# Gate product of an encoder block: one more k-pair of the second half formed by seven products, and three k-pairs held back to the end instead of four

## The chip, the cores and the metric

The kernel is one program on one core of a Trainium2 chip. The metric is the device time of one execution in microseconds (us), the median over several runs. All times inside an execution are counted from the start of its profiled span.

## The reference, cut to what matters

One layer of an encoder on x (256 tokens x 2048 channels, float32): a state-space and pooling mixer, a gated convolutional MLP, and last a gated embedding. Only this last step is touched:

```
gate = sigmoid(rmsnorm(h, ple_norm_pre) @ w_ple_gate)     # 256 x 2048 @ 2048 x 2048
h = h + rmsnorm(gate * (p @ w_ple), ple_norm_post)
```

## The kernel before, in words

**Stages.** In time order: input projection and mixer, output projection, the MLP's *up* product (11264 columns, 300 to 786 us), its *down* product (786 to 1008), and the *gate* product (from 1020). Each product runs in float32 accuracy by three passes: every operand x is split into a high part (a cast on ACT, line 153) and a low part (x minus the high part, on DVE, line 154), and PE adds high x high, high x low and low x high.

**The gate product** is `token_major`, called once for each half of the 1024 output columns (lines 1140 to 1152). The outputs of a half are four PSUM banks of 128 tokens x 512 columns, acc[t][o] for t = 0, 1 (tokens) and o = 0, 1 (columns). The 2048 input channels are 16 blocks of 128, taken in pairs: a pair k covers blocks k and k+1. `gt_ks` gives the order of the blocks, so u counts the pairs in that order.

- A *plain* pair is one load of 1 MB (`raw`, ring of three buffers), two splits of 128x1024 and 24 matmuls of 128x512 (2 blocks x 2 t x 2 o x 3 passes).
- A *fast* pair (`gt_fast` lists its u) is Winograd's form of a 2x2 block product: seven products instead of eight, 21 matmuls (`seven_products`, line 255). It needs two block sums of the weights and four sums of the activations. The weights' part that is needed as it is, 0.75 MB, goes to `raw` (tile gt18r for pair 8 of half 1), the block sums, 1 MB, to a *page* (gt18t). They are split in four pieces: a (128x512), b, d and c (128x1024 each). a and b come from r, d and c from t.
- After the last fast pair one more pair follows, and then `combine` (line 283) adds the products together on DVE and changes the accumulators in place. In half 1 it also cuts acc[1][1] in two outputs of 256 columns.
- With `tail` = n, the last n pairs are *held back*: their splits are made as they come, and their matmuls run at the end, output by output, so that the first tokens' outputs are complete while PE still works on the other tokens. In half 1 `tail` is 4.
- Held-back pairs must keep their splits. Those of the plain rings hold five tiles; for two of the four pairs of half 1 four pages are set aside (`spare`, lines 1148 to 1151).

**Block sums** are made during up (`block_sums`, line 226): a job fetches 1 MB of weights into a page (SP's queue), adds blocks in place on DVE (four additions of 128x512, line 253), and stores the page to DRAM (POOL's queue). The up product is cut in 176 pieces of 16 matmuls; the job with number i is fetched at piece `46 * i // 10 + 4` and added and stored three pieces later (lines 923 to 927). 37 jobs: 32 for down, 5 for gate. The last two in the list, those of the first two fast pairs of down, stay in their pages.

**Activations' sums** (`Sums`, line 808) are made on first use and kept, two pairs to a page: psp8 holds those of pairs 8 and 10, psp12 those of pair 12.

**Pages** are a pool of 13 tiles of 128x2048. A page is taken when its tile is first written and free after its last use, so the list of tiles also sets which load waits for what.

**The finish** (lines 1153 to 1178, `finish`, line 1119): for each output a tanh on ACT (L1163), a product with pl (L1164, DVE), the sum of squares (L1171, ACT) and a product with a gain (L1172, DVE). Here pl[0], the tile plb, serves half 0. When all outputs of a token group are there, POOL makes the reciprocal root (L378, L381) and DVE scales and adds h, four pieces of 512 (L1135). For the second token group the last output's sum of squares closes the norm (L1169, with a number from L1117), then POOL L1122, ACT L1126, one product on PE (line 1127, into the bank `gof` that line 1177 has filled with h), ACT L1129, and the stores.

**Order.** In up an order written out by hand (`in_order`) holds ACT, DVE and SP to the program's order. Elsewhere a scheduler orders each engine; each engine and each DMA queue then works in that order, so a load that waits for its buffer holds up the loads behind it.

Of the kernel before, what the change touches and what calls it, by code (L numbers as in the profile page):

```python
# [20 lines left out]
NK = D // P  # L21
# [32 lines left out]
def build(nc, a, out):  # L54
# [3 lines left out]
    w_down, w_gate, w_ple = a["w_down"], a["w_gate"], a["w_ple_"]  # L58
    out = out[0]

    with tile.TileContext(nc) as tc, \
# [21 lines left out]
        def main(name):  # L83
            return [pm.tile([P, 512], F32, tag="main", name=f"{name}_{i}") for i in range(2)]

        def misc(name):
            return pc.tile([P, 512], F32, tag="misc", name=name)

        def mm(o, lhsT, rhs, start, stop):
            last["pe"] = ins(nc.tensor.matmul(o, lhsT, rhs, start=start, stop=stop, skip_group_check=True))  # L90
# [15 lines left out]
        acc, acc2 = [main(f"dtu{t}") for t in range(2)], main("dtu2")  # L106
# [50 lines left out]
        def raw(name, src=None):  # L157
            r = wp.tile([P, 2048], F32, tag="raw", bufs=3, name=name)
            if src is not None:
                last["dma"] = load(r, src, True)  # L160
            return r
# [57 lines left out]
        def columns(acc):  # L219

            c = 0
            for o in acc:
                yield o, c
                c += o.shape[-1]
# [30 lines left out]
        def seven_products(name, stage, w, k0, c0, a_, acc, alt, start, stop):  # L255

            if (stage, c0, k0) in sums_:
                r = raw(f"{name}r")  # L260
                last["dma"] = load(r[:, 512:], w[c0 // 1024, k0 // 2][:, 512:], True)
                t, held = sums_[stage, c0, k0]
                if not held:
                    t = page(f"{name}t")
                    last["dma"] = load(t, sums_[stage, c0, k0][0], True)
            else:
                r = t = raw(f"{name}r", w[c0 // 1024, k0 // 2])
            b11 = split(f"{name}a", r[:, 512:1024], 512)
            b2 = split(f"{name}b", r[:, 1024:], 1024)
            if r is t:  # L270
                add_blocks(r)
            t42 = split(f"{name}d", t[:, 1024:], 1024)
            t31 = split(f"{name}c", t[:, :1024], 1024)

            for x, (wh, wl), c, o, own in (
                    ("a11", b11, 0, alt[0], True), ("a12", b2, 0, acc[0][0], False), ("a22", t42, 0, acc[1][0], False),
                    ("s4", b2, 512, acc[0][1], False), ("s2", t42, 512, alt[3], True), ("s1", t31, 512, alt[1], True),
                    ("s3", t31, 0, alt[2], True)):
                xh, xl = a_[x]
                for q, (xx, ww) in enumerate(((xh, wh), (xh, wl), (xl, wh))):  # L280
                    mm(o, xx, ww[:, c:c + 512], own and start and q == 0, own and stop and q == 2)
# [23 lines left out]
        def token_major(name, w, c0, ks, get, acc, tail=1, fast=(), alt=None, sums=None, at=()):  # L305


            group, nu = [], len(ks) // 2
            for u in range(nu):
                if u in at:  # L310
                    at[u]()
                k0 = ks[2 * u]
                if u in fast:
                    if u == fast[0]:
                        alt = alt + [misc(f"{name}s{i}") for i in (2, 3)]
                    seven_products(f"{name}{k0}", name[:2], w, k0, c0, sums(k0), acc, alt, u == fast[0], u == fast[-1])
                    continue
                r = None if f"{name}{k0}_0" in ready else raw(f"{name}r{k0}", w[c0 // 1024, k0 // 2])
                for j in range(2):
                    group.append((k0 + j, *split(f"{name}{k0}_{j}", r and r[:, j * 1024:(j + 1) * 1024], 1024)))  # L320
                if nu - tail <= u < nu - 1:
                    continue

                order = [(t, o, g, q) for t in range(2) for o in columns(acc[t]) for g in group for q in range(3)] \
                    if u == nu - 1 or u - 1 in fast[-1:] else \
                    [(t, o, g, q) for g in group for t in range(2) for q in range(3) for o in columns(acc[t])]
                for t, (o, c), (k, wh, wl), q in order:
                    xh, xl = (v[:, t * P:(t + 1) * P] for v in get(k))
                    xx, ww = ((xh, wh), (xh, wl), (xl, wh))[q]
                    c = (c + 512 * (k + 1)) % 1024  # L330
                    mm(o, xx, ww[:, c:c + o.shape[-1]], k == ks[0] and q == 0, k == ks[-1] and q == 2)
                if u - 1 in fast[-1:]:
                    combine(name, acc, alt, nu - tail == u + 1 and tail > 1)
                group = []
                aside()
            if nu in at:
                at[nu]()
# [116 lines left out]
        for u in range(0, NK, 2):  # L454
# [20 lines left out]
            for j in range(2):  # L475
# [3 lines left out]
                if k == 8:  # L479
                    half = last["act"], last["dve"]  # L480
# [428 lines left out]
            h_kept.append(dp.tile([P, D], F32, tag=f"h{t}", bufs=1, name=f"h_kept{t}"))  # L909
        pl_kept = dp.tile([P, D], F32, tag="pl", bufs=1, name="pl_kept")  # L910

        dn_fast, gt_fast = ((2, 3, 4, 5, 7, 8, 9, 10, 11, 12, 13, 14, 15, 16, 17, 18, 19), (2, 3, 4, 5, 7, 8, 9, 11, 12, 13, 14, 15, 16, 18, 19)), ((4, 5, 6), (1, 2))

        dn_stored = (2, 3, 5, 7, 8, 10, 11, 13, 14, 16, 17, 18, 19)
        gt_ks = list(range(NK)), [0, 1, 8, 9, 10, 11, 2, 3, 4, 5, 6, 7, 12, 13, 14, 15]
        which = [("dn", w_down, c * 1024, 2 * u) for c in range(2) for u in dn_fast[c]] + \
            [("gt", w_gate, c * 1024, gt_ks[c][2 * u]) for c in range(2) for u in gt_fast[c]]
        jobs_at = [[] for _ in range(NPIECES)]
# [3 lines left out]
        jobs_at[6].append(lambda: load(pl_kept, pl[0]))  # L922
        for i, w_ in enumerate(which[2:] + which[:2]):
            fetch, add, store = block_sums(*w_, i >= len(which) - 2)
            n = 46 * i // 10 + 4
            jobs_at[n].append(fetch)
            jobs_at[n + 3].extend((add, store))
        hid, kept = [], {}
# [87 lines left out]
        with in_order():  # L1016
            for _ in range(5):
                next_part()
            for n in range(NPIECES):
                s, v, i = blocks[n // 4]  # L1020
                if n % 4 == 0:
                    acc = main(f"{'gv'[v]}a{s}{i}")
# [60 lines left out]
        def first():  # L1083
# [3 lines left out]
            for j in range(2):  # L1087
# [4 lines left out]
        hp = sublayer("dn", w_down, list(range(NF)), hid_get, gload("gffn", a["ffn_norm_post"][0]), h, V_PN,  # L1092
                      fast=dn_fast, sums=hid_sums, at={11: first, NF // 2: lambda: (ple_parts(), back())}, row=rf)
# [45 lines left out]
        hps = Sums("ps", hp)  # L1139
        for half in range(2):  # L1140

            alt = [] if half else main(f"gts{half}")
            acc = [main(f"gt{half}{t}") for t in range(2)]
            alt += main(f"gts{half}") if half else []
            ks, fast = gt_ks[half], gt_fast[half]
            if half == 1:

                for i in (8, 10):
                    sh, sl = page(f"gth{i}", F32R), page(f"gtl{i}", F32R)
                    for j in range(2):  # L1150
                        spare[f"gt1{ks[i]}_{j}"] = (sh[:, j * 1024:(j + 1) * 1024], sl[:, j * 1024:(j + 1) * 1024])
            token_major(f"gt{half}", w_gate, half * 1024, ks, hp, acc, 1 + 3 * half, fast, alt, hps)
            for t in range(2):
                for n, (o, c0) in enumerate(columns(acc[t])):
                    c1 = c0 + o.shape[-1]
                    c = slice(half * 1024 + c0, half * 1024 + c1)

                    th = mid(f"gth{half}{t}{n}")
                    v = th[:, :c1 - c0]
                    end = half == t == 1 and c1 == 1024  # L1160
                    if end:
                        rest_of(th[:, c1 - c0:c1 - c0 + 1])
                    nc.scalar.activation(v, o, AF.Tanh, scale=rh[t])  # L1163
                    nc.vector.scalar_tensor_tensor(v, v, 1.0, pl[half][:, t * 1024 + c0:t * 1024 + c1],  # L1164
                                                   op0=ALU.add, op1=ALU.mult)
                    q = tiny(f"gq{t}{half}{n}", 1)
                    sv, so = (th[:, a_:a_ + c1 - c0 + end] for a_ in (0, 512))
                    if end:
                        nc.scalar.activation(so, sv, AF.Square, scale=D ** -0.5, accum_out=q)  # L1169
                    else:  # L1170
                        nc.scalar.activation(so, sv, AF.Square, accum_out=q)  # L1171
                    nc.vector.tensor_mul(vg[t][:, c], v, gple[:, c])  # L1172
                    sq[t].append(q)
                if half == 1:
                    if t == 0:
                        last_ps = misc("gof")
                        mm(last_ps, ident, h[1][:, :512], True, False)
                    finish(t)
# [72 lines left out]
```

## Time and profile before

| | us |
|---|---|
| runs, median (lowest to highest) | 1116.56 (1115.88 to 1116.61) |
| profiled execution | 1116.13 |
| its span, first to last instruction | 1114.4 |
| PE busy in the span | 1104.0 (99%) |
| DVE busy | 959.6 (86%) |
| ACT busy | 723.8 (65%) |
| POOL busy | 69.0 (6%) |

The time of an execution is some 1.7 us longer than its span. PE is TensorE, PEld its weight loads, DVE VectorE, ACT ScalarE, POOL GpSimd, SP the engine that issues most DMAs; a q behind a name (SPq) is the sequencer that issues or waits. A row of a timeline gives the start, the duration, the engine, the line of the kernel, the operation and `out<-in` with the tiles' names, where buffer numbers are left out: `gt` stands for all accumulators of the gate product, `gt1r` for the loads of plain pairs of half 1, `gt110t` for t of pair 10 of half 1. A bracket behind it names the idle time ahead of it and what ended that. Matmuls overlap, so PE's pace is the distance of their starts, not their durations.

### The profile page before, as it was taken

To read this page: it belongs to the slowest core of one execution; us is meant where nothing else is said; L and a number is where in the kernel's file an instruction comes from. 1 tells how busy PE (TensorE), PEld (TensorE's weight loads), DVE (VectorE), ACT (ScalarE), POOL (GpSimd) and SP (SyncE) were. 2 spreads that over 40 slices of the span, in tenths; PEclk is the share of its full clock that TensorE was granted. 3 is DMA by queue.
4 is the path that set the end of the run, shared out by engine and by line. 5 is a ranking of instruction groups with operands and counts; after the bars stand their busy time and mean duration, and the time that the engine had idled before them with its cause. 6 is when DMAs were issued, how large, how long until landed. Compare 5 with 4: busy or idle time off the path is not lost.

```text
span 1114.4 us, 16061 instructions
## 1 busy us (share of the span) xinstructions
PE 1104.0 (99%) x5964; PEld 950.6 (85%) x5964; DVE 959.6 (86%) x1338; ACT 723.8 (65%) x1056; POOL 69.0 (6%) x140
## 2 busy tenths in 40 slices
PE   9999999999999999999999999999999999999997
PEld 9999988888888888888888888888888888877876
DVE  6568997899868998888888888888899999989895
ACT  6858763555775565664655655657689878767673
POOL 0200000100100000000000000000000000001001
PEclk9999999999999999999999999999999999999999
DMA  9753346454589999999899999999999899995662
GB/s 363 314 204 137 117 188 263 151 189 178 195 343 397 382 396 385 361 378 374 335 378 385 356 377 366 352 393 391 362 382 381 322 348 403 415 378 222 265 235 105
DMA packets 54943, 347.29 MB, mean 312 GB/s; under 512 B 6096, under 2 KB 6992, under 8 KB 20176
## 3 DMA queue, kind: packets, MB, share of 16 engines
q1 hardware_dynamic: 44064, 289.53, 66.8%
q0 software_dynamic: 10368, 56.10, 13.3%
q8 instruction: 47, 0.77, 0.3%
q10 hardware_dynamic: 432, 0.62, 0.2%
q14 instruction: 32, 0.26, 0.1%
HBM read 297.48 MB, written 48.76 MB: 311 GB/s over the span
## 4 chain that ended last, share of the span: by engine, by line
PE 94%; DVE 2%; ACT 2%; issue 1%; POOL 1%; DMA 0%; SPq 0%; POOLq 0%; ACTq 0%
PE ga L90 22%; PE va L90 22%; PE dna L90 12%; PE woa L90 7%; PE xbc L90 5%; PE gt L90 5%; PE z L90 4%; PE dns L90 4%; PE dtu L90 4%; PE dn0s L90 2%; PE dn1s L90 2%; PE yd L90 1%; PE pw L90 1%; PE gts L90 1%; PE ple L90 1%
## 5 line engine op out<-in xcount | busy, mean ns | idle before, releaser
L90 PE MATMUL ga<-wox,ug_0h 128*128 128x512 f32 x352 | 125.5, 395 | 0.0
L90 PE MATMUL ga<-wox,ug_1h 128*128 128x512 f32 x352 | 125.1, 394 | 0.0
L90 PE MATMUL va<-wox,uv_1h 128*128 128x512 f32 x352 | 124.8, 393 | 0.0
L90 PE MATMUL va<-wox,uv_0h 128*128 128x512 f32 x352 | 124.8, 393 | 0.0
L90 PE MATMUL ga<-wox,ug_1l 128*128 128x256 f32 x352 | 99.1, 282 | 0.0
L90 PE MATMUL va<-wox,uv_1l 128*128 128x256 f32 x352 | 99.1, 281 | 0.0
L90 PE MATMUL va<-wox,uv_0l 128*128 128x256 f32 x352 | 99.1, 281 | 0.0
L90 PE MATMUL ga<-wox,ug_0l 128*128 128x256 f32 x352 | 99.0, 281 | 0.0
L253 DVE TENSOR_TENSOR dnb<-dnb 128x512 f32<-128x512 f32 x128 | 88.3, 690 | 3.1
L90 PEld LDWEIGHTS va<-wox,uv_1h 128*128 128x128 f32 x352 | 66.1, 188 | 15.0
L90 PEld LDWEIGHTS ga<-wox,ug_1h 128*128 128x128 f32 x352 | 66.1, 188 | 15.0
L90 PEld LDWEIGHTS va<-wox,uv_0h 128*128 128x128 f32 x352 | 66.1, 188 | 15.0
L90 PEld LDWEIGHTS ga<-wox,ug_0h 128*128 128x128 f32 x352 | 66.1, 188 | 14.9
L90 PEld LDWEIGHTS ga<-wox,ug_0l 128*128 128x128 f32 x352 | 66.2, 188 | 0.1
L90 PEld LDWEIGHTS ga<-wox,ug_1l 128*128 128x128 f32 x352 | 66.2, 188 | 0.0
L90 PEld LDWEIGHTS va<-wox,uv_0l 128*128 128x128 f32 x352 | 66.2, 188 | 0.0
L90 PEld LDWEIGHTS va<-wox,uv_1l 128*128 128x128 f32 x352 | 66.2, 188 | 0.0
L937 ACT CAST hs<-hid 128x512 fp32r<-128x512 f32 x44 | 27.3, 621 | 21.8 <-PE dna L90 21.6
L244 POOL DMA_DIRECT2D dns<-dnb x30 | 16.2, 541 | 310.9 <-DVE dnb L253 310.9
L938 DVE TENSOR_TENSOR hs<-hid,hs 128x512 fp32r<-128x512 f32 x44 | 30.2, 686 | 5.8 <-ACT hs L937 5.8
L801 ACT CAST he<-he 128x512 fp32r<-128x512 f32 x13 | 8.1, 621 | 37.7 <-DVE he L800 37.7
L90 PE MATMUL dna<-dn_1h,hs 128*128 128x512 f32 x96 | 30.9, 393 | 0.0
(2247 smaller groups left out, 3227.7 us busy)
## 6 DMA issues: line engine op xcount, KB each, us to landing
dnb<-w_down SPq DMA_DIRECT2D x32, 1024.0 KB, 9.8
dns<-dnb POOLq DMA_DIRECT2D x30, 1024.0 KB, 6.6
hd<-hsum POOLq DMA_DIRECT2D x24, 512.0 KB, 8.3
zr<-w_z SPq DMA_DIRECT2D x8, 1024.0 KB, 4.9
dtur<-w_dtu SPq DMA_DIRECT2D x14, 528.0 KB, 8.6
wo0r<-w_out_ SPq DMA_DIRECT2D x7, 1024.0 KB, 4.9
dn1r<-w_down SPq DMA_DIRECT2D x7, 1024.0 KB, 6.8
hsum<-he POOLq DMA_DIRECT2D x13, 512.0 KB, 7.7
```

The source lines that it names most:

```text
L90: last["pe"] = ins(nc.tensor.matmul(o, lhsT, rhs, start=start, stop=stop, skip_group_check=True))
L244: nc.gpsimd.dma_start(t, pg[0])
L253: nc.vector.tensor_add(v[:, i], v[:, i], v[:, j])
L801: nc.scalar.copy(o[:, :512], s[:, :512])
L937: nc.scalar.copy(t[:, :512], hid_part(k))
L938: nc.vector.tensor_sub(t[:, 512:], hid_part(k), t[:, :512].bitcast(F32))
```

## The change

```
-        dn_fast, gt_fast = (...), ((4, 5, 6), (1, 2))
+        dn_fast, gt_fast = (...), ((4, 5, 6), (1, 2, 3))
...
-        gt_ks = list(range(NK)), [0, 1, 8, 9, 10, 11, 2, 3, 4, 5, 6, 7, 12, 13, 14, 15]
+        gt_ks = list(range(NK)), [0, 1, 8, 9, 10, 11, 12, 13, 2, 3, 4, 5, 6, 7, 14, 15]
...
-            n = 46 * i // 10 + 4
+            n = 45 * i // 10 + 4
...
-                for i in (8, 10):
+                for i in (10,):
                     sh, sl = page(f"gth{i}", F32R), page(f"gtl{i}", F32R)
                     for j in range(2):
                         spare[f"gt1{ks[i]}_{j}"] = (sh[:, j * 1024:(j + 1) * 1024], sl[:, j * 1024:(j + 1) * 1024])
-            token_major(f"gt{half}", w_gate, half * 1024, ks, hp, acc, 1 + 3 * half, fast, alt, hps)
+            token_major(f"gt{half}", w_gate, half * 1024, ks, hp, acc, 1 + 2 * half, fast, alt, hps)
```

In half 1 of the gate product the pairs now run 0; 8, 10, 12 as fast pairs; 2; and 4, 6, 14 held back. Before, they ran 0; 8, 10 fast; 2; and 4, 6, 12, 14 held back. The block sums of pair 12 for these columns are one job more in up (38), and the jobs stand 45 instead of 46 tenths of a piece apart. Its activations' sums are those that half 0 has already made (psp12). One held-back pair instead of two keeps its splits in pages, the other two in the rings.

More of the change, by code (lines that the diff above doesn't have):

```diff
@@ L910, in build @@
         pl_kept = dp.tile([P, D], F32, tag="pl", bufs=1, name="pl_kept")
-        dn_fast, gt_fast = ((2, 3, 4, 5, 7, 8, 9, 10, 11, 12, 13, 14, 15, 16, 17, 18, 19), (2, 3, 4, 5, 7, 8, 9, 11, 12, 13, 14, 15, 16, 18, 19)), ((4, 5, 6), (1, 2))
+        dn_fast, gt_fast = ((2, 3, 4, 5, 7, 8, 9, 10, 11, 12, 13, 14, 15, 16, 17, 18, 19), (2, 3, 4, 5, 7, 8, 9, 11, 12, 13, 14, 15, 16, 18, 19)), ((4, 5, 6), (1, 2, 3))
         dn_stored = (2, 3, 5, 7, 8, 10, 11, 13, 14, 16, 17, 18, 19)
-        gt_ks = list(range(NK)), [0, 1, 8, 9, 10, 11, 2, 3, 4, 5, 6, 7, 12, 13, 14, 15]
+        gt_ks = list(range(NK)), [0, 1, 8, 9, 10, 11, 12, 13, 2, 3, 4, 5, 6, 7, 14, 15]
         which = [("dn", w_down, c * 1024, 2 * u) for c in range(2) for u in dn_fast[c]] + \
```

## The prediction

> **What bounds the kernel now.** I read the end of the chain of work that ended last first, then the busy time by stretches, then the waits of PE in two of them.
>
> ```profile
> 741.62 22.33 PE ga L90 x128
> ...
> 1077.63 16.75 PE gt L90 x73
> ...
> 1099.12 2.75 DVE vg L1135 x4
> 1101.87 0.61 DVE gth L1164
> ...
> 1103.23 0.37 ACT gth L1163
> ...
> 1103.62 0.44 DVE gth L1164
> ```
> ```profile
> 300.00:786.00 486.00, 486.00 (x2790) 426.50 (x2789) 417.20 (x576) 294.06 (x444) 28.35 (x54) 1.00 0.95 373
> ...
> 1069.00:1094.00 25.00, 25.00 (x110) 20.42 (x111) 22.76 (x25) 14.58 (x16) 0.00 (x0) 1.00 0.50 169
> 1094.00:1114.40 20.40, 13.30 (x77) 10.66 (x75) 10.40 (x17) 6.98 (x17) 4.48 (x9) 0.90 0.31 104
> ```
> ```profile
> PE gt L90 <- DVE gt18bl L154: 0.4, 1, 0.4
> ```
>
> The stretches show length, then busy time of PE, PEld, DVE, ACT and POOL, granted clock, DMA share and GB/s. PE carries the chain until 1094.4; it is full in up (300 to 786) and in the second half of the gate product (1069 to 1094). After 1094.4 the chain leaves PE: the finishing work of the first 128 tokens runs over ACT, POOL and DVE, then that of the other 128. The last fence is the whole list of PE's waits between 1060 and 1105; the same list for up is empty. So the change can act in three places: on DVE and DMA in up, on PE's unbroken stretch from 1069 to 1094, and on the finish.
>
> **Up.** It gains one fetch (1 MB, SP), four additions on DVE and one store (1 MB, POOL's queue).
>
> ```profile
> L253 DVE TENSOR_TENSOR dnb<-dnb 128x512 f32<-128x512 f32 x128 | 88.3, 690 | 3.1
> ```
>
> One job is 4 x 0.69 = 2.8 us of DVE, which is free for 486 - 417 = 69 us here; 2 MB at 373 GB/s are under 6 us of a stretch with a DMA share of 0.95. The jobs also close up, from 46 to 45 tenths of a piece: by that formula the first five stay at pieces 4, 8, 13, 17 and 22, those between come one to three pieces earlier, and the two kept for down's start come one later, the last additions at piece 173 instead of 172. I cost this at nothing. What hides it is PE's work, 22.33 us for each 128 matmuls without a gap; without that cover one job's 2.8 us is the price. In down PE, ACT and POOL keep their order; some SP loads swap with a neighbour.
>
> **PE in the second gate half.** Pair 12 now takes 21 matmuls of 128x512 instead of 24.
>
> ```profile
> 1077.46 0.40 PE L90 MATMUL gt<-gt_0h,dnxh 128*128 128x512 f32 x1
> ...
> 1082.99 0.40 PE L90 MATMUL gt<-gth,dnxh 128*128 128x512 f32 x1
> ...
> 1093.97 0.39 PE L90 MATMUL gt<-gt_1h,dnxl 128*128 128x512 f32 x1
> ...
> 1094.66 0.39 PE L90 MATMUL gt<-gt_1h,dnxl 128*128 128x512 f32 x1
> ...
> 1099.45 0.28 PE L90 MATMUL gt<-gth,dnxh 128*128 128x256 f32 x1
> 1099.57 0.28 PE L90 MATMUL gt<-gtl,dnxh 128*128 128x256 f32 x1
> ```
>
> Pair 2's 24 matmuls start from 1077.46 to 1082.99, so a step is 0.230 us and the saving 3 x 0.23 = **0.69 us**. The held-back group now begins at 1077.46 + (21 + 24) x 0.230 = 1087.83. Before, it is 72 full steps (1082.99 to 1099.45, 0.2286 each) and 48 of half width (0.12); after, 54 full ones, the matmul of line 1177 (`gof`) that the scheduler now puts among them, and 36 of half width. So PE ends 0.69 - 0.23 = 0.46 us earlier.
>
> **What feeds PE.** The queue of loads decides here.
>
> ```profile
> 1059.68 0.33 SPq L120 DMA_DIRECT2D gt1r<-w_gate  x1
> 1060.12 0.37 SPq L120 DMA_DIRECT2D gt18t<-gts  x1
> 1060.54 0.42 SPq L120 DMA_DIRECT2D gt110t<-gts  x1
> ```
> ```profile
> gt1r<-w_gate SPq DMA_DIRECT2D x5, 1024.0 KB, 4.9
> gt18t<-gts SPq DMA_DIRECT2D x1, 1024.0 KB, 7.7
> gt110t<-gts SPq DMA_DIRECT2D x1, 1024.0 KB, 9.8
> ```
> ```profile
> 1065.76 0.68 DVE L1164 SCALAR_TENSOR_TENSOR gth<-gth,plb 128x512 f32<-128x512 f32 x1
> ...
> 1067.56 1.22 DVE L154 TENSOR_TENSOR gt18bl<-gt18r,gt18bh 128x1024 fp32r<-128x1024 f32 x1
> ...
> 1070.15 1.22 DVE L154 TENSOR_TENSOR gt18cl<-gt18t,gt18ch 128x1024 fp32r<-128x1024 f32 x1
> 1071.29 0.68 DVE L154 TENSOR_TENSOR gt110al<-gt110r,gt110ah 128x512 fp32r<-128x512 f32 x1
> 1071.89 1.22 DVE L154 TENSOR_TENSOR gt110bl<-gt110r,gt110bh 128x1024 fp32r<-128x1024 f32 x1
> 1073.02 1.22 DVE L154 TENSOR_TENSOR gt110dl<-gt110t,gt110dh 128x1024 fp32r<-128x1024 f32 x1
> ...
> 1084.15 0.42 DVE L301 TENSOR_TENSOR gts<-gt,gt1v 128x256 f32<-128x256 f32 x1
> 1084.49 1.21 DVE L154 TENSOR_TENSOR gtl<-gt1r,gth 128x1024 fp32r<-128x1024 f32 x1
> ```
> ```profile
> 1071.30 1.05 ACT L153 CAST gt110dh<-gt110t 128x1024 fp32r<-128x1024 f32 x1
> ```
>
> The activations' sums of pair 12 (a page, `psp12`) now live until this half. In the built program gt110t therefore takes the page of pl[0] (`plb`), read last by the L1164 of 1065.76, and the new gt112t takes the page of gt18t, free when gt18cl is split. SP's order becomes gt112r, gt18t, gt110t, gt1r of pair 2, gt112t, then pairs 4, 6, 14. So gt110t leaves at about 1066.45 instead of 1060.54. Behind it waits pair 2's load, but that also needs gt18r's buffer (gt18bl, until 1068.8) as before; gt112t leaves at about 1071.2. The three issues at 1059.68 to 1060.54 landed 4.9, 7.7 and 9.8 us after issue, in order: about 4.9 us alone, 2.5 to 3.3 us more for each load queued ahead. I take 4.9 for gt110t (nothing left ahead) and 5.3, about 1076.5, for gt112t (pair 2's load, issued at 1068.8, is mostly through). The bounds are 4.9 and 9.8.
>
> From start to start DVE takes 1.13 us for a 128x1024 split and 0.60 for a 128x512. Pair 12 costs it 0.60 + 3 x 1.13 instead of 2 x 1.13, 1.7 us more in a stretch with 22.8 of 25 us busy. With gt110t landed at 1071.4 its ACT cast (1.05) ends by 1072.5, before DVE comes to it at 1073.0: nothing is late. gt112's d part: cast until 1077.6, split until 1078.8; PE takes the high half at 1077.46 + 7 x 0.23 = 1079.07, the low half at 1080.45. Its c part is ready at 1080.0 (due 1081.6), pair 2's at 1081.1 and 1082.2 (due 1082.8 and 1083.9). Then DVE has the combination, which can begin at 1084.6, when PE has left the first output: six operations of 0.60, two of half width at 0.34 and, among and behind them, five splits of 1.13. It has pair 14's low halves at 1093.4 and 1094.5; PE, in the new order, takes them at 1094.4 and 1095.6. So PE never waits, but everywhere with about 1 us in hand; a load 1 us late costs nothing, each further us costs one.
>
> **The finish.** Three held-back pairs instead of four also mean less PE work after the first tokens are done.
>
> ```profile
> 1095.41 0.69 ACT L1163 ACTIVATE gth<-gt,rh 128x512 f32<-128x512 f32 x1 [0.32 <-ACT gth L1163]
> ...
> 1104.41 0.19 ACT L1171 ACTIVATION_READ_ACCUMULATOR gth<-gth 128x1 f32 x1
> ...
> 1105.41 0.47 ACT L1163 ACTIVATE gth<-gts,rh 128x256 f32<-128x256 f32 x1 [0.82 <-PE gts L90]
> ...
> 1106.44 0.42 ACT L1169 ACTIVATE gth<-gth 128x257 f32<-128x257 f32 x1 [0.55 <-DVE gth L1164]
> ```
>
> The first tokens' two halves ended on PE at 1093.97 and 1094.66; now at 1087.83 + 35 and 40 x 0.2286 = 1095.83 and 1096.97, **1.9 and 2.3 us later**. The scaling of L1135 follows at the same distance: 1101.0 to 1101.4 instead of 1099.12. From there to the sum that ends at 1104.60 it was 5.5 us; the new order lifts one L1163 and one L1164 of the other tokens (0.37 + 0.44 in the chain) ahead of that sum, so 4.6 to 4.7: 1105.6 to 1106.1. Before, ACT then waited 0.82 for PE, until 1105.41; now PE is done at about 1104.9 and ACT is the late one. So L1163, and all behind it, come 0.2 to 0.7 us later than at 1105.41. **I take 0.45 later**; PE's gain is lost because the finish no longer hides beside it.
>
> **The sum.** Against the profiled execution: 1116.13 us (span 1114.4) + 0.45 = 1116.6. That execution lies 0.4 under the median of the runs, 1116.56; against the median it is **1117.0 us**. About 0.2%, 2.2 us, is what a measurement of this kernel tells from no change.
>
> **Rivals.**
> - *PE's end decides.* If the finish catches up, PE's 0.46 us are gained: 1116.1. For it: the 0.82 us that ACT waited for PE. Against: 2 us less cover.
> - *gt112t late.* With 7.7 us, as gt18t had, it lands at 1078.9; the cast ends at 1080.0 instead of the due 1079.07: 1 us, 1118.0.
> - *gt110t late: slower.* It leaves 5.9 us later than before, by the wait for pl[0]'s page. With 9.8 us, as before, it lands at 1076.2; its cast ends at 1077.3, due at 1074.0 on PE: 3.3 us stall, and the same page queue behind it: 1117.0 + 3.3 = 1120.3. It decides from a landing over 6 us (due 1072.5). Against: what was ahead of it then is gone. The Trainium skill, page "DMA: Bandwidth & Descriptors", section "Two DMAs through the same engine are not ordered", says that nothing orders DMAs across the 16 engines; by it pair 2's load could delay gt110t although issued later. The trace so far speaks against it: the three landed in the order of issue.
> - *Up is not covered.* A job's 2.8 us fall on PE where a piece has a sum job too: 1119.8.
> - *Faster.* The closer jobs spare a wait that I don't see; PE has only 0.4 us of waits here, so over 2.2 us has no place in these rows.
>
> **How the numbers follow.** Forecast (1116.4 to 1117.6) 0.54, PE's end 0.10, gt112t late 0.10, gt110t late 0.13, up 0.08, faster 0.05. Within 0.2% are the first three, 0.74; slower 0.21; faster 0.05. The range takes the first three and up, 0.82, with 0.4 us for the spread of runs below: 1115.6 to 1119.8.
>
> **What would show it.** Right: gt110t leaves near 1066.4, gt112t near 1071.2; PE unbroken from 1068.8 to the last half-width matmul; the first tokens' L1163 about 1.9 us later; ACT without a wait for PE before the last L1163. Wrong: a PE wait on gt110dh or gt112dh (late loads), any PE wait in up, or ACT still waiting for PE at the last L1163.

## The result and the profile after

The changed kernel takes 1117.73 us (median of 21 runs, 1117.27 to 1118.74), the kernel before in the same measurement 1116.19 (21 runs, 1115.74 to 1116.68). The ratio is 1.0014, with a 95% interval of 1.0008 to 1.002. So the change costs 1.5 us. The prediction had 1117.0 us, 0.45 above the kernel before; the sign and the place were right, the size was three times too small. The profiled execution took 1118.05 us, its span 1116.3.

Two executions don't start alike. The first product of pair 8 (`gts<-gt18ah`) is a mark ahead of everything that the change touches in this half; first its row in the kernel before, then in the changed kernel:

```profile
1067.07 0.39 PE L90 MATMUL gts<-gt18ah,dnxh 128*128 128x512 f32 x1
```
```profile
1067.57 0.39 PE L90 MATMUL gts<-gt18ah,dnxh 128*128 128x512 f32 x1
```

Half a microsecond of the span's 1.9 is there already. It is no part of the change: up is the first stage that the change touches, and its first product (`ga<-wox,ug_0h`) already starts at 292.01 us instead of 291.47. From there to the mark it is 775.6 us in both. The variants of the kernel before have the mark anywhere from 1067.15 to 1067.79 in their own profiled executions below. **All differences below are counted from this mark**, so 0.50 is taken off the changed kernel's times. From the mark to the end of the span it is 47.3 us before and 48.7 after: 1.4 us, which agrees with the medians.

The same stretches as in the prediction (length, then busy time of PE, PEld, DVE, ACT and POOL, granted clock, DMA share, GB/s), after:

```profile
300.00:786.00 486.00, 486.00 (x2791) 426.60 (x2790) 419.86 (x581) 294.98 (x443) 28.87 (x55) 1.00 0.96 377
1069.00:1094.00 25.00, 24.67 (x105) 19.81 (x106) 23.06 (x27) 15.82 (x18) 0.00 (x0) 1.00 0.64 245
1094.00:1116.30 22.30, 14.13 (x72) 10.89 (x71) 11.77 (x19) 6.85 (x17) 4.20 (x9) 0.83 0.28 95
```

PE is full in up, with 2.66 us more of DVE work beside it, and full in the gate stretch but for the wait that was there before (next fence; it now ends behind 1069.00). The list of PE's waits from 1060 to 1107:

```profile
PE gt L90 <- DVE gt18bl L154: 0.4, 1, 0.4
```

So no load is late. The loss is all in the third stretch. PE and the feeding of it, in the timeline after:

```profile
1066.96 0.33 SPq L120 DMA_DIRECT2D gt110t<-gts  x1
1069.34 0.33 SPq L120 DMA_DIRECT2D gt1r<-w_gate  x1
1071.58 0.32 SPq L120 DMA_DIRECT2D gt112t<-gts  x1
...
1078.15 1.05 ACT L153 CAST gt112dh<-gt112t 128x1024 fp32r<-128x1024 f32 x1 [2.72 <-PE gt1s L90]
...
1079.59 0.39 PE L90 MATMUL gt<-gt112dh,dnxh 128*128 128x512 f32 x1
...
1088.37 0.40 PE L90 MATMUL gt<-gth,dnxh 128*128 128x512 f32 x1
...
1091.10 1.02 PE L90 MATMUL gof<-hb,ident 128*128 128x512 f32 x2
...
1097.04 0.39 PE L90 MATMUL gt<-gt_1h,dnxl 128*128 128x512 f32 x1
...
1098.20 0.40 PE L90 MATMUL gt<-gt_1h,dnxl 128*128 128x512 f32 x1
...
1105.78 0.28 PE L90 MATMUL gts<-gt_1h,dnxl 128*128 128x256 f32 x1
```

And the chain of work that ended last, from the first tokens' last output on (start, length, engine, tile, line):

```profile
1091.26 0.86 PE gof L90 x2
1092.12 5.33 PE gt L90 x23
...
1102.08 2.74 DVE vg L1135 x4
...
1105.46 0.73 ACT gth L1171 x2
1106.36 0.28 POOL go1m L1115
...
1106.93 0.53 POOL go1m L1115
1107.54 0.74 POOL gth L1117
```

The chain leaves PE at 1097.47 and doesn't come back until the last product. Before, it went through the same L1135 but had a second way at its end: L1169 waited for the last L1163 and L1164, which had waited for PE. Now L1169 waits for L1117 on POOL, and that is the new wait:

```profile
1106.40 0.19 ACT L1171 ACTIVATION_READ_ACCUMULATOR gth<-gth 128x1 f32 x1
1106.49 0.45 ACT L1163 ACTIVATE gth<-gts,rh 128x256 f32<-128x256 f32 x1
1106.98 0.43 DVE L1164 SCALAR_TENSOR_TENSOR gth<-gth,pl 128x256 f32<-128x256 f32 x1 [0.28 <-ACT gth L1163]
...
1108.31 0.42 ACT L1169 ACTIVATE gth<-gth 128x257 f32<-128x257 f32 x1 [1.36 <-POOL gth L1117]
...
1109.48 2.08 DVE L1135 SCALAR_TENSOR_TENSOR vg<-vg,go1r,hb 128x512 f32<-128x512 f32 x3 [1.61 <-POOL go1r L1122]
```

L1163 has no wait for PE any more, as the prediction said, and begins at 1105.99 on the clock of before (1105.41 then): 0.58 later. L1169 begins at 1107.81 on that clock (1106.44 then): 1.37 later. The second number is the loss.

### The profile page after: what moved, and what is told of

The parts are those of the page before. It is cut to its first block, busy times and chain, and to the rows that moved or that the text cites. A ratio compares the mean times of both kernels' runs of the same rounds, so it can differ in the third digit from the quotient of the medians.

```text
span 1116.3 us, 16061 instructions
## 1 busy us (share of the span) xinstructions
PE 1104.4 (99%) x5955; PEld 950.6 (85%) x5955; DVE 963.6 (86%) x1344; ACT 725.3 (65%) x1058; POOL 68.4 (6%) x141
## 4 chain that ended last, share of the span: by engine, by line
PE 94%; DVE 2%; ACT 1%; DMA 1%; POOL 0%; issue 0%; POOLq 0%; ACTq 0%
PE ga L90 22%; PE va L90 22%; PE dna L90 12%; PE woa L90 7%; PE xbc L90 5%; PE gt L90 4%; PE z L90 4%; PE dns L90 4%; PE dtu L90 4%; PE dn0s L90 2%; PE dn1s L90 2%; DMA dtur<-w_dtu 1%; PE gts L90 1%; PE yd L90 1%; PE pw L90 1%; PE ple L90 1%
## 5 line engine op out<-in xcount | busy, mean ns | idle before, releaser
L90 PE MATMUL dna<-dn_0h,hs 128*128 128x512 f32 x96 | 30.6, 395 | 0.3 <-ACT dn_0h L153 0.3
```

## The experiments

All times are medians of 11 runs, beside 27 or 33 runs of the kernel before on the same chip (in the row of the changed kernel 21 and 21). The third column after the names is the distance from the mark to the end of the span in the one profiled execution of each.

| kernel | median, us | less before beside it | mark to end, us | ratio to before, 95% interval |
|---|---|---|---|---|
| before | | | 47.3 | |
| changed | 1117.73 | +1.54 | 48.7 | 1.0008 to 1.002 |
| e2_up_only | 1116.49 | +0.19 | 47.3 | 0.9992 to 1.0009 |
| e1_gof_last | 1117.56 | +1.26 | 48.5 | 1.0002 to 1.002 |
| e5_keep_warm | 1117.75 | +1.45 | 48.7 | 1.0004 to 1.0021 |
| e4_before_gof_early | 1117.17 | +0.87 | 48.2 | 0.9999 to 1.0017 |
| e3_three_held | 1116.99 | +0.64 | 47.8 | 0.9996 to 1.0014 |
| e6_dve_order | 1116.82 | +0.47 | 47.7 | 0.9994 to 1.0012 |
| e8_both | 1115.89 | -0.46 | 46.8 | 0.9987 to 1.0005 |
| e9_before_order | 1116.67 | +0.32 | 47.5 | 0.9993 to 1.0011 |
| e11_sum_left_out | 1117.06 | +0.71 | 47.9 | 0.9997 to 1.0014 |
| e12_before_extra_sum | 1116.34 | -0.01 | 47.3 | 0.9991 to 1.0009 |
| e13_after_extra_sum | 1118.10 | +1.75 | 49.0 | 1.0006 to 1.0025 |

One interval is some 1 us to each side, so a single median doesn't settle half a microsecond. The distance from the mark, which the profile gives apart from any difference at the start, agrees with every difference of medians within some 0.2 us, and the rows show where it arises. How well it repeats can be seen in the three kernels whose work behind the mark is the same or nearly so (before, e2_up_only, e12_before_extra_sum): 47.25 to 47.33 us.

My first theory was that the product of line 1177 (`gof`) carries half of the loss or more: it stands among the held-back matmuls, takes 0.86 us there, and at the end PE's granted clock had fallen for the last product (2.08 us instead of 1.12). The first four runs test it and the cost of up.

**Up alone.**

```
+        which.append(("gt", w_gate, 1024, 12))
-            n = 46 * i // 10 + 4
+            n = 45 * i // 10 + 4
```

> The kernel before, with only up's part of the change: pair 12's block sums for the second half are made and stored as a 38th job, jobs 45 instead of 46 tenths of a piece apart; nothing reads the extra sums. Theory: up hides it, no PE wait there, within 0.3 us of the kernel before. Rival (up pays): 1 to 3 us above the kernel before, and PE waits between 300 and 786 us.

It came out 0.19 us above the kernel before by the medians, and the list of PE's waits between 300 and 786 us is empty. The distance from the mark says nothing of up, which lies ahead of it; the length of up does. From up's first product to the first product of down it is 494.59 us here (291.97 to 786.56), 494.60 in the changed kernel (292.01 to 786.61) and 494.64 before (291.47 to 786.11). From there to the mark, through down with its swapped loads, it is 280.93, 280.96 and 280.96. The stretch from 300.5 to 786.5 us here:

```profile
300.50:786.50 486.00, 486.00 (x2789) 426.52 (x2789) 419.87 (x580) 294.34 (x443) 28.96 (x55) 1.00 0.96 377
```

DVE has the same 419.9 us of work as in the changed kernel, and PE doesn't miss a step. Up pays nothing.

**The product of line 1177 back at the end.**

```
-                        mm(last_ps, ident, h[1][:, :512], True, False)
+                        with tc.issue_after(last["pe"]):
+                            mm(last_ps, ident, h[1][:, :512], True, False)
```

> The changed kernel, with the product of line 1177 (gof<-hb,ident) held back until after the last held-back matmul, where it stood before the change. Theory (the loss sits in the finish, and half or more of it is this product): the first tokens' last matmuls come 0.2 and 0.4 us earlier, those of the second tokens 0.86 us earlier, PE's idle time ahead of the last product falls from 3.9 to about 2 us and that product's row from 2.08 to about 1.1 us; in all 1.2 to 1.6 us less than the changed kernel, within 0.4 us of the kernel before. Rival (up's extra job or the later loads are the cost): within 0.3 us of the changed kernel, 1.2 to 1.6 us above the kernel before. Rival (less cover alone, the last product's speed being chance): 0.4 us less than the changed kernel.

Only 0.2 to 0.3 us came back, where I had expected 1.2 to 1.6. The theory falls; the rival with 0.4 us is the nearest. The timeline of this run shows why:

```profile
1101.95 2.75 DVE L1135 SCALAR_TENSOR_TENSOR vg<-vg,go0r,hb 128x512 f32<-128x512 f32 x4 [1.16 <-POOL go0r L381]
...
1103.20 0.47 ACT L1163 ACTIVATE gth<-gt,rh 128x256 f32<-128x256 f32 x1 [1.51 <-PE gt L90]
1104.62 1.01 DVE L1164 SCALAR_TENSOR_TENSOR gth<-gth,pl 128x512 f32<-128x512 f32 x2
...
1108.17 0.42 ACT L1169 ACTIVATE gth<-gth 128x257 f32<-128x257 f32 x1 [1.36 <-POOL gth L1117]
```

The second tokens' outputs leave PE 0.9 us earlier, counted from the mark (L1163 at 1103.20, 1104.05 in the changed kernel), and then lie, because DVE is in the four scalings of L1135 until 1104.70. Only the first tokens' own gain, about 0.2 us, gets through.

**PE kept at work before the last product.** One more product of the same form behind the last held-back matmul, into a bank already read; its result goes nowhere.

```
+                    else:
+                        with tc.issue_after(last["pe"]):
+                            mm(acc[0][0], ident, h[1][:, 512:1024], True, True)
```

> The changed kernel, with one more product of the same form (hb x ident, 128x512) behind the last held-back matmul, into a bank that has been read by then; its result is not used. The product of line 1177 stays where the change put it. Theory: PE's idle time ahead of the last product falls by about 0.9 us and that product takes about 1.1 instead of 2.08 us, so the time is 0.7 to 1.0 us less than that of the changed kernel. Rival (the last product is slow for another reason, its operands or the stores beside it): its row stays at about 2.1 us and the time within 0.2 us of the changed kernel.

The last product took 1.70 instead of 2.08 us, not the 1.1 that I expected, and the time stayed as it was. So the last product is off the path, although the list of the chain runs its last steps over it. The end of the span follows the start of the last three scalings (L1135, x3) by 6.8 us in the kernel before (1107.61 to 1114.4), in the changed one (1109.48 to 1116.3) and here (1109.44 to 1116.2), whether that product takes 1.12, 2.08 or 1.70 us; in all thirteen profiled executions of this study it is 6.7 to 6.8. Those scalings wait for L1122, which waits for L1169, so what counts is when L1169 begins.

**The product early in the kernel before.**

```
+                for i, (t, (o, c), (k, wh, wl), q) in enumerate(order):
+                    if hook and u == nu - 1 and i == 12:
+                        hook()
```

> The kernel before, with the product of line 1177 put among the held-back matmuls (after the twelfth of them in the program's order) instead of behind them. Theory: everything behind it on PE comes 0.86 us later, and the last product of PE stands after a longer idle time and takes about 2.1 instead of 1.1 us: 0.9 to 1.9 us above the kernel before. Rival (the place of this product doesn't matter, or costs 0.23 us as the prediction had it): 0 to 0.3 us above the kernel before.

The hook issues the product of line 1177, and the line itself goes. It costs 0.87 us, the product's own length and the lower end of what I expected; the last product took 1.79 us, but it is off the path (line numbers are higher here: L1171 is L1163 of the kernel before):

```profile
1088.86 1.02 PE L90 MATMUL gof<-hb,ident 128*128 128x512 f32 x2
...
1106.48 0.47 ACT L1171 ACTIVATE gth<-gts,rh 128x256 f32<-128x256 f32 x1 [1.37 <-PE gts L90]
```

In the kernel before ACT waits for PE at the last L1163, so all 0.86 us are paid; in the changed kernel nobody waits for PE there, so the same product is nearly free. The price of an instruction is that of the path it stands on.

That left the chain from the first tokens through L1135 to the sums, as the second theory. Four runs test it.

**DVE's order at the end.** ACT, DVE and SP hold to the program's order in the last part; `finish(0)` only puts the four scalings of the first tokens on a list, and they are issued between the products of the others. The product with a gain (L1172) of each of the others' outputs but the last now follows behind the L1164 of the next.

```
+                    scaled.append(lambda c=c: scale(c))
...
+              with in_order() if half == t == 1 else nullcontext():
...
+                        for f in (scaled[:2], scaled[2:3], scaled[3:])[n]:
+                            f()
```

> The changed kernel, with the four scalings of the first tokens (L1135 of t=0) no longer in one block of 2.74 us on VectorE ahead of the other tokens' products: ScalarE and VectorE run the end in a written order, two scalings behind the first L1164 of t=1, one behind the second, one behind the third. The product of line 1177 stays where the change put it. Theory (the chain from the first tokens' last matmul through their scaling to the other tokens' sums sets the end, and the sums of L1115 and L1117 on GpSimd stand at its end): the second sum is ready 0.8 us earlier or more, L1169 follows L1164 again and not L1117, and the time is 0.8 to 1.3 us less than that of the changed kernel. Rival (the serial work on GpSimd itself or PE's end sets it): within 0.3 us of the changed kernel.

1.07 us came back by the medians (1.0 from the mark). With nine lines more ahead of them, L1172 is L1163 here, L1173 is L1164, L1178 L1169, L1116 and L1118 are L1115 and L1117, L1136 is L1135, and L1184 is L1172:

```profile
1102.80 1.41 DVE L1136 SCALAR_TENSOR_TENSOR vg<-vg,go0r,hb 128x512 f32<-128x512 f32 x2
...
1105.77 0.47 ACT L1172 ACTIVATE gth<-gts,rh 128x256 f32<-128x256 f32 x1 [0.62 <-PE gts L90]
1106.09 0.55 POOL L1118 TENSOR_TENSOR gth<-go1m,half_up 128x1 f32<-128x1 f32 x1
...
1106.80 0.42 ACT L1178 ACTIVATE gth<-gth 128x257 f32<-128x257 f32 x1 [0.55 <-DVE gth L1173]
```

ACT waits for PE again, and the sums are there 0.16 us before they are needed. The path is back on PE.

**Both.** The written order, and the product of line 1177 at the end.

> As the run before, and the product of line 1177 behind the last held-back matmul as well. Theory: with the scalings out of the way PE's end decides, and this product is then worth its 0.86 us: 0.6 to 0.9 us less than the run with the written order alone, 1.5 to 2.1 us less than the changed kernel, 0.2 to 0.6 us under the kernel before (three matmuls fewer). Rival (this product's place is worth nothing anywhere): within 0.2 us of the run with the written order alone.

Its edits are those of e6_dve_order and e1_gof_last. Now the product is worth 0.93 us by the medians (1116.82 to 1115.89), where it was worth 0.2 to 0.3 without the order:

```profile
1104.99 0.47 ACT L1172 ACTIVATE gth<-gts,rh 128x256 f32<-128x256 f32 x1 [0.62 <-PE gts L90]
...
1106.01 0.42 ACT L1178 ACTIVATE gth<-gth 128x257 f32<-128x257 f32 x1 [0.55 <-DVE gth L1173]
```

The mark is at 1067.32 here, 0.25 later than before, so the last L1163 begins at 1104.74 on the clock of before, 0.67 earlier than there: the three matmuls that pair 12 saves. This is the fastest kernel of the study, 2.0 us under the changed one by the differences to before. Against the kernel before it has 0.46 us by the medians and by the mark, but its interval holds 1, so that gain is not secured by the times alone.

**Three held back, without more seven products.** The kernel before with 4 in plain order instead of held back; the cut of the last bank stays.

```
-            token_major(f"gt{half}", w_gate, half * 1024, ks, hp, acc, 1 + 3 * half, fast, alt, hps)
+            token_major(f"gt{half}", w_gate, half * 1024, ks, hp, acc, 1 + 2 * half, fast, alt, hps)
...
-                for i in (8, 10):
+                for i in (10,):
```

Two more lines of the edit, not shown, make `combine` cut the last bank although pair 4 still follows, and let pair 4 run output by output as pair 2 does.

> The kernel before with three pairs held back and no seventh-product pair more: pairs 8 and 10 by seven products, then 2 (cut in three outputs as before) and 4 in plain order, 6, 12 and 14 held back, one of them in pages. PE has as many matmuls as before and ends at the same time. Theory (less work held back costs cover): the first tokens' last matmul comes 1.9 us later, the other tokens' sums about 1 us later, L1169 waits for L1117; 0.6 to 1.4 us above the kernel before, so about the changed kernel's time. Rival (seven products, their loads or the extra job cost the time, not the number held back): within 0.3 us of the kernel before.

0.64 us slower with the same matmuls by the medians, its lowest expected value, and 0.45 from the mark. The product of line 1177 stands at 1105.16 on the clock of before (1105.15 there), so PE's end is where it was, and L1169 waits for L1117 here too:

```profile
1100.53 2.75 DVE L1135 SCALAR_TENSOR_TENSOR vg<-vg,go0r,hb 128x512 f32<-128x512 f32 x4 [1.15 <-POOL go0r L381]
...
1105.41 1.02 PE L90 MATMUL gof<-hb,ident 128*128 128x512 f32 x2
...
1107.25 0.42 ACT L1169 ACTIVATE gth<-gth 128x257 f32<-128x257 f32 x1 [0.90 <-POOL gth L1117]
```

So the smaller group alone turns the end from PE to this chain, and is worth 0.5 to 0.6 of the 1.5 us. L1135 begins 1.3 us earlier here than in the changed kernel (1100.53 - 0.25 against 1102.08 - 0.50); the last matmul of the first tokens' second output stands 1.14 earlier (1096.81 - 0.25 against 1098.20 - 0.50). By the count of steps it is the 36th of the group here; there the product of line 1177 (0.86) and four matmuls of other outputs (0.92) stand ahead of it too, and pair 12 saves 0.69: 1.09 of the 1.14.

**The written order in the kernel before.** The same edit as in e6_dve_order.

> The kernel before with the written order of the end (scalings of the first tokens spread between the other tokens' products), nothing else. Theory: there ScalarE waits for PE at the last L1163 (0.82 us), so the order is worth nothing: within 0.3 us of the kernel before. Rival (the block of scalings sets the end before as well): 0.5 to 1.0 us under the kernel before.

No gain: 0.3 us slower by the medians, 0.2 from the mark, which the interval doesn't tell from nothing. The order is worth something only where the chain through L1135 decides.

**One sum less, one operation more.** The last three runs take the step that I now held for the wrong one: what L1169 waits for. First the changed kernel without the second to last output's sum in the norm; it leaves that part out of the computation.

```
-            for n, q in enumerate(sq[1]):
+            for n, q in enumerate(sq[1][:-1]):
```

> The changed kernel, with the sum of squares of the second to last output left out of the norm of the other tokens (one L1115 less on GpSimd, in front of L1117), so the output is not the reference's. Theory (L1169 waits for L1115 and L1117 behind the late sum, not for the last L1163): L1169 then follows L1164 by 0.55 us of idle time as before the change, 0.6 to 0.9 us earlier, and the time falls by as much, to about what the prediction had for the changed kernel. Rival (L1163 and L1164 set the end, as the prediction had it): within 0.2 us of the changed kernel.

0.83 us less than the changed kernel by the differences to before:

```profile
1106.81 0.55 POOL L1117 TENSOR_TENSOR gth<-go1m,half_up 128x1 f32<-128x1 f32 x1
1106.87 0.43 DVE L1164 SCALAR_TENSOR_TENSOR gth<-gth,pl 128x256 f32<-128x256 f32 x1 [0.27 <-ACT gth L1163]
...
1107.39 0.42 ACT L1169 ACTIVATE gth<-gth 128x257 f32<-128x257 f32 x1 [0.56 <-POOL gth L1117]
```

L1164 and L1117 end within 0.06 us of each other, and L1169 begins 0.57 later than before on the clock of before, which is L1163's 0.58. This is what the prediction had priced: everything but the sums on POOL.

Then one operation more of 128x1 on POOL ahead of L1117, in both kernels.

```
+            m = tiny("go1x", 1)
+            nc.gpsimd.tensor_scalar(m, base, 1.0, 0.0, op0=ALU.mult, op1=ALU.add)
```

> The kernel before, with one more operation on GpSimd between the last L1115 and L1117 (times 1 plus 0, on 128x1). Theory: L1117 ended 0.78 us before L1169 began, one more operation of 0.27 to 0.55 us fits into that: within 0.2 us of the kernel before. Rival (every GpSimd operation ahead of L1169 is paid): 0.3 to 0.6 us more.

> The same operation more in the changed kernel. Theory: nothing hides it there, 0.3 to 0.6 us above the changed kernel. Rival (L1163 and L1164 set the end): within 0.2 us of the changed kernel.

Nothing in the kernel before (47.3 us from the mark), 0.2 us by the medians and 0.3 from the mark in the changed one. The rows of the operation and of L1169 (L1171 in these two); first the kernel before with it, then the changed one with it:

```profile
1105.21 0.19 POOL L1118 TENSOR_SCALAR go1x<-go1m 128x1 f32<-128x1 f32 x1
...
1106.52 0.42 ACT L1171 ACTIVATE gth<-gth 128x257 f32<-128x257 f32 x1 [0.55 <-DVE gth L1166]
```
```profile
1107.55 0.37 POOL L1118 TENSOR_SCALAR go1x<-go1m 128x1 f32<-128x1 f32 x1
...
1108.59 0.42 ACT L1171 ACTIVATE gth<-gth 128x257 f32<-128x257 f32 x1 [1.64 <-POOL gth L1119]
```

The wait for POOL grows from 1.36 to 1.64 us in the changed kernel; in the other the operation vanishes in the slack. That is a little less than the 0.3 to 0.6 expected in time, but on the side of the theory in the trace.

## Why the prediction was right and where it wasn't

**The number: inside the range, in part by luck.** 1117.73 lies within 1115.6 to 1119.8, but just outside the band that I gave the forecast itself (1116.4 to 1117.6). The range reached further only for rivals that didn't come about: "gt112t late" had 1118.0, but PE has no wait on gt112dh, so that it is near is chance. As a difference the forecast was 0.45 us and the result 1.5; and 1117.0 stood on a median of 1116.56 for the kernel before, where 21 runs give 1116.19.

**Up costs nothing: right.** e2_up_only shows it alone, by the length of up.

**The held-back group's start: right.** Forecast 1087.83; 1088.37 less 0.50 is 1087.87.

**The product of line 1177: mis-sized.** I took it for one matmul step, 0.23 us. It is 0.86 in the chain. Its row stood in the trace of before, where the product lay at the end:

```profile
1105.15 1.02 PE L90 MATMUL gof<-hb,ident 128*128 128x512 f32 x2
```

Two records and 1.02 us say that it is not a step like the others. Its operands are plain float32, where the split operands are fp32r. The Trainium skill, page "FP8 and Floating Point Precision", section "TensorE Precision Notes", says that true FP32 takes four passes through the array; by that rule it would be four steps, an estimate of 4 x 0.23 = 0.92, and the trace agrees with 0.86. So PE ended not 0.46 us earlier but 0.24 later: its last matmul starts at 1105.78 - 0.50 = 1105.28, before at 1105.04 (the second row; it stands ahead of that product):

```profile
1105.04 0.28 PE L90 MATMUL gts<-gt_1h,dnxl 128*128 128x256 f32 x1
```

It cost little here, since PE's end no longer decided.

**Feeding: right, with less in hand.** gt110t left at 1066.46 on the clock of before (forecast 1066.45) and gt112t at 1071.08 (1071.2). The changed kernel's DMA issues, with the median time to landing:

```profile
gt110t<-gts SPq DMA_DIRECT2D x1, 1024.0 KB, 4.9
gt112t<-gts SPq DMA_DIRECT2D x1, 1024.0 KB, 6.5
```

gt110t took the 4.9 us that I gave it. gt112t took 6.5 and not 5.3, and 5.7 to 6.4 in the six other runs with these loads. Pair 2's load had been issued 2.2 us ahead of it, pair 4's 1.7 behind it; which of them delayed it was not taken apart. Its cast ended at 1079.20, and PE took the high half at 1079.59, so 0.4 us were left instead of the 1.5 of my working. (The row of the cast names PE, which ended a product at 1078.12, when the load landed too. In e1_gof_last the same cast waits for the load and begins before PE starts that product.) Both rivals of late loads are refuted; the one with gt112t was close. What the rival on gt110t cites from the Trainium skill, that nothing orders DMAs over the engines, did no harm to gt110t in this execution.

**The finish: right up to its last step.** The first tokens' last matmuls started at 1097.04 and 1098.20, on the clock of before 2.6 and 3.0 us later instead of 1.9 and 2.3; the mis-sized product is 0.63 of the 0.7 in each; L1135 came 2.46 later; the reading of the late sum ended at 1106.59 - 0.50 = 1106.09, and the forecast was 1105.6 to 1106.1; L1163 came 0.58 later, and the forecast was 0.2 to 0.7. The step that failed is the sentence *"So L1163, and all behind it, come 0.2 to 0.7 us later than at 1105.41"*. What is behind it doesn't hang on L1163 alone. L1169 squares 256 products and one number more, the one that L1117 makes on POOL out of the sums. Before, L1117 was ready 0.78 us ahead of L1169:

```profile
1104.76 0.27 POOL L1115 TENSOR_SCALAR go1m<-gq,go1m 128x1 f32<-128x1 f32 x1 [1.10 <-ACT gth L1171]
1105.11 0.55 POOL L1117 TENSOR_TENSOR gth<-go1m,half_up 128x1 f32<-128x1 f32 x1
```

I had followed the sum to its reading and there compared it with ACT's next free moment; the 1.06 us from the reading's end (1104.60) to L1117's end (1105.66) I left out. The chain of before, which the prediction quotes as far as L1164 at 1103.62, goes on in the same view to just these two operations. The sum came 1.49 us later, and the way from its reading to L1117's end took 1.69 us instead of 1.06, so 0.63 more. Less the slack of 0.78 that is 1.34 of the 1.37 us by which L1169 came later. It is 0.8 more than L1163's 0.58, and e11_sum_left_out takes just that away.

The reorder that I counted as a relief has a part in the 0.63: the two late sums are now read 0.4 us apart, so POOL has two L1115 in a row ahead of L1117. But the second L1115 begins only 0.18 later behind its reading than before (0.34 instead of 0.16); the rest is that it takes 0.53 us instead of 0.27 and L1117 0.74 instead of 0.55.

**Rivals.** That PE's end decides was right for e6_dve_order and e8_both and wrong for this kernel: it needs DVE's order changed. The end came later than forecast, but not by a late load.

## What to carry to other kernels

When a change shortens the work that covers a finishing chain, follow every operand of the instruction at which the ways meet, the 128x1 operations on GpSimd too, and write down each one's slack in the trace of before; the one with the least slack past its own delay sets the new end. A block of long operations that only feeds stores (here four scalings of 2.74 us together) should not stand ahead of the short ones on the path: spread between them it cost nothing, and the three saved matmuls showed. And the same instruction had a price of 0.2 to 0.3 us in the changed kernel and of 0.9 in the kernel before and in the one with the written order, by the path that it stood on, so a part is to be undone alone and together with the part that hides it.

## What the runs showed of the hardware that I had not expected

The granted TensorE clock fell to half while PE had nothing to do, but not a fixed time after its last matmul. The changed kernel ended its held-back matmuls at 1106.06 and was at half clock from 1108.5 on; the kernel before ended the product of line 1177 at 1106.17, ran its last one at 1108.06, and was still at full clock up to 1110. A stretch each of the kernel before and then of the changed one (the granted clock is the third number from the end):

```profile
1109.50:1110.00 0.50, 0.00 (x0) 0.00 (x0) 0.19 (x1) 0.31 (x1) 0.00 (x0) 1.00 0.98 361
```

```profile
1108.50:1109.00 0.50, 0.00 (x0) 0.00 (x0) 0.00 (x0) 0.32 (x2) 0.10 (x1) 0.52 0.00 0
```

The product that fell behind that point took 2.08 us instead of 1.12, and e5_keep_warm, with 0.9 us less of idle time, still met the drop (1.70). The idle time alone doesn't set it. e13_after_extra_sum ended its held-back matmuls at 1106.06 like the changed kernel, and was at full clock up to 1109.5, a microsecond longer. After 2.06 us of idle time the last product took 1.71 us in e8_both; after 2.92 us it took 1.13 in e6_dve_order. The Trainium skill, page "TensorE: Matmul & The Clock Gate", section "Part 1: The HAM clock gate (the "warmup" mystery)", tells of a free-running window of activity of about 3.4 us, and of half clock after at least one idle window. A window that is not tied to the last matmul fits these rows, but a drop after 2.4 us is earlier than one idle window of that length. What sets it was not tried further, since the product lies off the path.

A 128x1 operation on GpSimd had no fixed time: L1117 took 0.55 us before and in e11_sum_left_out, 0.74 in the changed kernel; the operation added in the last two runs took 0.19 and 0.37. In the longer cases DVE was in L1172 (L1174 in the last two runs) at the time (1107.44 to 1107.86 in the changed kernel), in the shorter ones not. That the one slows the other is argued from these rows and was not tried by itself.
